# Buffers for turned and flat planes in a hybrid decoder layer: four and three in place of two and four

## The chip, the cores and the metric

The kernel runs on one core of one Trainium2 chip. The metric is device time in microseconds of one execution; lower is better. Before the change the median of three runs is 2429.04 us (2428.55 to 2429.09).

## What is computed

One decoder layer over 256 tokens of width 2048, all in float32: a SwiGLU, two token mixers in parallel (retention and sliding-window attention), a second SwiGLU, and a final RMS norm. A conditioning vector `c` gives nine rows of shifts, scales and gates by the product with `w_ada`.

```python
def token_mixing(h, w_in, w_ret_branch, w_swa_branch, w_out, sinks):
    rq, rk, rv, rg, sq, sk, sv, gl_ret, gl_swa = jnp.split(h @ w_in, IN_SPLITS, axis=-1)
    ...
    ro = retention_chunkwise(rq, rk, rv)
    ro = ro * lax.rsqrt(jnp.mean(ro * ro, axis=-1, keepdims=True) + NORM_EPS)
    ro = (jax.nn.silu(rg.astype(jnp.float32)) * ro.reshape(b, s, RET_V_W)).astype(h.dtype)
    y_ret = ro @ w_ret_branch
    so = swa_with_sinks(...)
    y_swa = so @ w_swa_branch
    merged = jax.nn.sigmoid(gl_ret) * y_ret + jax.nn.sigmoid(gl_swa) * y_swa
    return merged @ w_out

def reference(x, c, w_ada, ...):
    c_act = jax.nn.silu(c)
    for l in range(DEPTH):
        mod = (c_act @ w_ada[l] + b_ada[l]).reshape(b, N_MOD, D_MODEL)
        h = modulate(rms_norm(x, norm_ffn1[l]), mod[:, 0], mod[:, 1])
        x = x + 0.5 * mod[:, 2][:, None, :] * swiglu(h, w_ffn1_gu[l], w_ffn1_down[l])
        h = modulate(rms_norm(x, norm_mix[l]), mod[:, 3], mod[:, 4])
        x = x + mod[:, 5][:, None, :] * token_mixing(h, ...)
        h = modulate(rms_norm(x, norm_ffn2[l]), mod[:, 6], mod[:, 7])
        x = x + 0.5 * mod[:, 8][:, None, :] * swiglu(h, w_ffn2_gu[l], w_ffn2_down[l])
    return rms_norm(x, norm_final)
```

## The kernel before

**Products.** Every float32 factor is split into a high part (`wh` of a weight, `hh` or `a` of an activation) and the rest (`wl`, `hl` or `a`), and each product is made of three: high by high, rest by high, high by rest (L342, L343, L344). Weights come as tiles `raw` of 128 x 4 x 512 (1 MB, L327, four buffers). Each is split in two pieces of 128 x 1024: ACT casts the high part (L350), DVE subtracts it from the raw tile for the low part (L352), into three buffers each. A piece feeds 12 matmuls: two rows of weights, two halves of the tokens, three products. A chunk of 512 output columns of a 2048-deep product takes 96 matmuls. The branch products take their activations from a slot and split them in pairs as they go: ACT casts (L385), DVE subtracts (L386), into the pool `asp` with two buffers.

**Turning.** Results with tokens on partitions have to be turned before the next product. Most are turned by DMA, in halves of 16 bits. `turn_by_dma` has three steps: `apart` copies the low and the high 16-bit words of a 128 x 512 tile into two flat planes on ACT (L452, pool `flat`); `turn` has SP issue a transpose for each plane (L458, pool `back`); `together` weaves the two turned planes back into the 32-bit destination on ACT (L466). The steps are spread over the weight loads that follow: `later` puts the two token halves of a chunk at steps 1 and 2 (`apart`), 6 and 7 (`turn`) and 9 (`together`), one step for each weight tile, and there are four tiles to a chunk, so the transposes of a chunk stand just behind the first `together` of the chunk ahead. `later_by_pairs` does the same for the four merged tiles of the first half of the branches: all four `apart` at once, and then pair by pair.

**Conditioning.** Beside the products DVE multiplies rows of `w_ada` with `silu(c)` and sums them (L206), four passes of 512 columns to a load of 1 MB (L201). In the mixing part these loads share the four `raw` buffers with the weights.

**Order.** SP's instructions stay in the order in which they are written. Those of PE, DVE and ACT are put in order by the framework, which plays the program through a model of the engines, buffers included, while it builds it; on the chip each engine then takes its list strictly in turn. POOL issues a few loads (gates, constants) from a scratch of descriptors in SBUF.

**Stages**, by the trace: the first SwiGLU to about 770 us, the norm and the way into mixing to 880, window queries, retention queries and keys to about 1090, retention values to 1150, gates and the retention gate to 1327, the branch products of the first half to about 1418, gates to 1509, branch products of the second half to 1600, then `w_out`, and the second SwiGLU from about 1720.

## Time and profile before

| what | us |
|---|---|
| median of three runs | 2429.04 |
| the profiled execution | 2432.27 |
| its span in the profile | 2430.5 |
| PE busy | 2379.1 |
| DVE busy | 1702.6 |
| ACT busy | 1284.1 |
| POOL busy | 5.6 |

The profile is of one execution; its span runs from the first to the last instruction. The engines are PE (matmuls), DVE (vector), ACT (scalar), POOL, and SP, which issues the loads; a row names the line of the kernel, the tile written and the tiles read. "SPq" is SP's queue: its waits are times in which it stood at the head of its list. Busy shares are means over the whole span; what a change in one stage is worth is read from that stage.

### The profile page before, as it was taken

Reading aid. Unit: us, or ns where it says so; the run is one execution under the profiler, and the core shown is the slowest. Engines: PE = TensorE matmul, PEld = TensorE weight load, DVE = VectorE, ACT = ScalarE, POOL = GpSimd, SP = SyncE. Lnnn points to the kernel's source line nnn. Section 1 sums busy time; section 2 is a strip of 40 time slices with the busy share of each in tenths; the row PEclk is TensorE's granted clock in tenths of the full one; section 3 lists DMA queues with packets and bytes.
Section 4 is the critical chain, followed back from the end, with each engine's and each line's share of the span. In section 5 each row is a group of like instructions: output and inputs, shape, how many; then the busy total and the mean of one; then the engine's idle time right before and its main releaser. Section 6 shows DMA issues by size and latency. Waiting matters only on the chain.

```text
span 2430.5 us, 28957 instructions
## 1 busy us (share of the span) xinstructions
PE 2379.1 (98%) x10686; PEld 1938.2 (80%) x10686; DVE 1702.6 (70%) x2741; ACT 1284.1 (53%) x1778; POOL 5.6 (0%) x14
## 2 busy tenths in 40 slices
PE   6999999999999999999999999999999999999998
PEld 4778888888787787778888788887788888888886
DVE  6998787778877668886666676767655555545656
ACT  5544545454545456665555554446555445454544
POOL 0000000000000000000000000000000000000000
PEclk9999999999999999999999999999999999999999
DMA  9988689998875677675677878755687777765563
GB/s 339 338 328 286 217 310 319 363 320 303 304 267 191 242 245 240 210 259 206 241 246 238 278 236 302 277 190 191 214 246 241 242 248 244 256 226 191 185 200 121
DMA packets 305008, 613.76 MB, mean 253 GB/s; under 512 B 70561, under 2 KB 70945, under 8 KB 286049
## 3 DMA queue, kind: packets, MB, share of 16 engines
q1 hardware_dynamic: 303362, 605.25, 73.3%
q0 software_dynamic: 928, 5.61, 0.6%
q8 instruction: 84, 1.38, 0.2%
q10 hardware_dynamic: 576, 1.05, 0.1%
q14 instruction: 58, 0.48, 0.1%
HBM read 595.06 MB, written 2.12 MB: 246 GB/s over the span
## 4 chain that ended last, share of the span: by engine, by line
PE 88%; DVE 4%; ACT 1%; issue 1%; DMA 1%; DVEq 0%; ACTq 0%
PE pa L344 28%; PE pa L343 28%; PE pa L342 28%; DVE wl L352 1%; PE ps L436 1%; ACT wh L350 1%; DMA raw<-in_w_ada_dram 1%; DVE slot L206 1%; DVE t L553 0%; PE pd L960 0%; PE pd L956 0%; DVE slot L874 0%; DVE raw L206 0%; PE ps L1029 0%; ACT hh L562 0%
## 5 line engine op out<-in xcount | busy, mean ns | idle before, releaser
L352 DVE TENSOR_TENSOR wl<-raw,wh 128x1024 fp32r<-128x1024 f32 (+1 forms) x828 | 994.0, 1207 | 584.2 <-ACT wh L350 578.8
L350 ACT CAST wh<-raw 128x1024 fp32r<-128x1024 f32 (+1 forms) x828 | 859.1, 1041 | 976.6 <-PE pa L343 936.1
L342 PE MATMUL pa<-wh,hh 128*128 128x512 f32 x2224 | 870.5, 393 | 3.6 <-ACT wh L350 3.1
L343 PE MATMUL pa<-wh,hl 128*128 128x512 f32 x2224 | 868.6, 391 | 2.4 <-DVE hl L527 1.9
L344 PE MATMUL pa<-wl,hh 128*128 128x512 f32 x2224 | 796.4, 392 | 4.0 <-DVE wl L352 3.7
L344 PEld LDWEIGHTS pa<-wl,hh 128*128 128x128 f32 x2224 | 415.5, 188 | 98.6 <-DVE wl L352 10.6
L342 PEld LDWEIGHTS pa<-wh,hh 128*128 128x128 f32 x2224 | 417.9, 188 | 93.5 <-ACT wh L350 5.0
L343 PEld LDWEIGHTS pa<-wh,hl 128*128 128x128 f32 x2224 | 418.2, 188 | 91.4 <-DVE hl L527 2.6
L343 PE MATMUL pa<-wh,a 128*128 128x512 f32 x992 | 385.3, 390 | 3.5 <-DVE a L386 3.5
L342 PE MATMUL pa<-wh,a 128*128 128x512 f32 x992 | 368.2, 391 | 3.1 <-DVE t L570 1.2
L344 PE MATMUL pa<-wl,a 128*128 128x512 f32 x992 | 367.7, 391 | 0.7 <-DVE wl L352 0.6
L342 PEld LDWEIGHTS pa<-wh,a 128*128 128x128 f32 x992 | 186.5, 188 | 44.0 <-DVE t L570 1.9
L343 PEld LDWEIGHTS pa<-wh,a 128*128 128x128 f32 x992 | 186.9, 188 | 42.9 <-DVE a L386 4.4
L344 PEld LDWEIGHTS pa<-wl,a 128*128 128x128 f32 x992 | 186.5, 188 | 41.0 <-DVE wl L352 2.5
L206 DVE CUSTOM_DVE_ANT_0 slot<-slot,cact 128x512 f32<-128x512 f32 (+1 forms) x252 | 192.8, 813 | 15.4 <-DMA slot<-in_w_ada_dram 15.1
L206 DVE CUSTOM_DVE_ANT_0 raw<-raw,cact 128x512 f32<-128x512 f32 (+1 forms) x260 | 167.1, 695 | 42.6 <-DMA raw<-in_w_ada_dram 30.9
L386 DVE TENSOR_TENSOR a<-slot,a 128x512 fp32r<-128x512 f32 x124 | 84.8, 685 | 14.0 <-ACT a L385 14.0
L385 ACT CAST a<-slot 128x512 fp32r<-128x512 f32 x124 | 76.4, 618 | 14.8 <-PE pa L344 14.7
L466 ACT COPY slot<-back 128x512 uint16<-128x512 uint16 x112 | 74.8, 766 | 0.0
L452 ACT COPY flat<-t 128x512 uint16<-128x512 uint16 x104 | 59.1, 618 | 7.9 <-DVE t L1088 6.3
L206 DVE DVE_READ_ACCUMULATOR2_ANT sums<- 128x1 f32 x512 | 41.9, 82 | 0.0
L486 ACT ACTIVATE pd<-x_sb 128x512 f32<-128x512 f32 x32 | 19.0, 593 | 35.8 <-DVE x_sb L571 32.2
(167 smaller groups left out, 986.6 us busy)
## 6 DMA issues: line engine op xcount, KB each, us to landing
raw<-in_w_ffn_gu_dram SPq DMA_DIRECT2D x152, 1024.0 KB, 5.3
raw<-in_w_in_dram SPq DMA_DIRECT2D x104, 1024.0 KB, 5.6
raw<-in_w_ffn_down_dram SPq DMA_DIRECT2D x88, 1024.0 KB, 5.2
slot<-in_w_ada_dram SPq DMA_DIRECT2D x76, 1024.0 KB, 7.5
raw<-in_w_ada_dram SPq DMA_DIRECT2D x64, 1024.0 KB, 5.9
raw<-in_w_ffn_gu_dram SPq DMA_DIRECT2D x24, 768.0 KB, 6.4
raw<-in_w_swa_branch_dram SPq DMA_DIRECT2D x16, 1024.0 KB, 6.0
raw<-in_w_ret_branch_dram SPq DMA_DIRECT2D x16, 1024.0 KB, 5.2
```

Source lines behind the costliest of these rows:

```text
L206: nc.vector.tensor_tensor_reduce(out=w[:, at], in0=w[:, at], in1=cact[:, at], scale=1.0, scalar=0.0, op0=ALU.mult, op1=ALU.add, accum_out= ...
L342: nc.tensor.matmul(ps, ah[:, j, ts], wh[:, j, :], start=first, stop=False)
L343: nc.tensor.matmul(ps, al[:, j, ts], wh[:, j, :], start=False, stop=False)
L344: nc.tensor.matmul(ps, ah[:, j, ts], wl[:, j, :], start=False, stop=last)
L350: cast.append(nc.scalar.copy(hi, src).ins)
L352: nc.vector.tensor_sub(lo, src, hi.bitcast(F32))
L385: nc.scalar.copy(hi, v)
L386: nc.vector.tensor_sub(lo, v, hi.bitcast(F32))
L436: nc.tensor.transpose(ps[:, j * P : (j + 1) * P], src_of(j), ident)
L452: nc.scalar.copy(planes[:, i, :], words(src)[:, :, i])
L466: nc.scalar.copy(into[:, :, :, i], held["turned"][:, i])
L486: nc.scalar.activation(side_bank(), src, AF.Square, accum_out=dest)
```

## The change

Pool `flat` has three buffers in place of four and pool `back` four in place of two. `turn_by_dma` takes a pool and a tag for its flat planes, which are now a float32 tile of 128 x 512 seen as two planes of 16 bits; the four merged tiles take theirs from the pool of 512-column tiles (`tmp`, tag `t512`, five buffers). The scratch for POOL's descriptors is 2048 in place of 4096 bytes. A flat and a `back` buffer are 2 KB a partition each.

```diff
-    flat = ctx.enter_context(tc.tile_pool(name="flat", bufs=4))
-    back = ctx.enter_context(tc.tile_pool(name="back", bufs=2))
+    flat = ctx.enter_context(tc.tile_pool(name="flat", bufs=3))
+    back = ctx.enter_context(tc.tile_pool(name="back", bufs=4))
...
-    def turn_by_dma(dest, src):
+    def turn_by_dma(dest, src, pool=flat, tag="flat"):
...
         def apart():
-            planes = flat.tile([P, 2, CH], U16, tag="flat", name=nm("flat"))
+            planes = pool.tile([P, CH], F32, tag=tag, name=nm("flat"))
+            planes = planes.bitcast(U16).rearrange("p (i n) -> p i n", i=2)
             with tc.issue_after(cast[-1]):
...
                 if p == 0:
-                    work.append(turn_by_dma(dest, m))
+                    work.append(turn_by_dma(dest, m, tmp, "t512"))
                     continue
...
-    nc = _bacc.Bacc("TRN2", target_bir_lowering=False, num_devices=1, dynamic_dma_scratch_size=4096)
+    nc = _bacc.Bacc("TRN2", target_bir_lowering=False, num_devices=1, dynamic_dma_scratch_size=2048)
```

The number of instructions of each kind and the order on SP and POOL stay as they are; lines below L450 are one further on. What moves is what SP's transposes wait for, and the order on PE, DVE and ACT from the window queries on.

SP where the sliding-window branch begins, before, with the semaphores that each row waits for (DMAHW: the landing of an earlier DMA; DVE, Activation: those engines' progress; `back_10687` and `back_10736` are the turned planes of the third chunk of the retention gate):

```order
L327 DMA raw_10651<-in_w_swa_branch_dram 128x4x512 [waits DMAHW6_49,DMAHW0_49,DVE_49]
L458 DMA_TRANSPOSE back_10687<-flat_10468 128x4x128 [waits DMAHW7_49,Activation_49]
L458 DMA_TRANSPOSE back_10687<-flat_10468 128x4x128
L327 DMA raw_10699<-in_w_swa_branch_dram 128x4x512 [waits DMAHW4_49,DMAHW1_49,DVE_49]
L201 DMA raw_10733<-in_w_ada_dram 128x2048 [waits DMAHW3_49,DMAHW2_49,DVE_49]
L458 DMA_TRANSPOSE back_10736<-flat_10512 128x4x128 [waits Activation_49]
```

The same rows of the change:

```order
L327 DMA raw_10651<-in_w_swa_branch_dram 128x4x512 [waits DMAHW6_49,DMAHW4_49,DVE_49]
L459 DMA_TRANSPOSE back_10687<-flat_10468 128x4x128 [waits DMAHW7_49]
L459 DMA_TRANSPOSE back_10687<-flat_10468 128x4x128 [waits DMAHW0_49]
L327 DMA raw_10699<-in_w_swa_branch_dram 128x4x512 [waits DMAHW1_49,DVE_49]
L201 DMA raw_10733<-in_w_ada_dram 128x2048 [waits DMAHW3_49,DMAHW2_49,DVE_49]
```

The transposes stand where they stood and no longer wait for ACT.

DVE at the same place, before; `raw_10733` is the conditioning load of SP's rows, `t_10591` and `t_10594` are the last chunk of the retention gate:

```order
L1167 TENSOR_TENSOR t_10591<-t_10591,slot_8209 128x512
L352 TENSOR_TENSOR wl_10654<-raw_10651,wh_10653 128x1024
L1167 TENSOR_TENSOR t_10594<-t_10594,slot_8209 128x512
L352 TENSOR_TENSOR wl_10671<-raw_10651,wh_10670 128x1024
L352 TENSOR_TENSOR wl_10702<-raw_10699,wh_10701 128x1024
L206 ISA raw_10733,sums_10800<-raw_10733,cact 128x512
L206 ISA sums_10800 128x1
L352 TENSOR_TENSOR wl_10718<-raw_10699,wh_10717 128x1024
```

The other three passes and then the two activation pairs (L386) follow. Now, from the last pass on:

```order
L206 ISA raw_10733,sums_10800<-raw_10733,cact 128x512
L206 ISA sums_10800 128x1
L1168 TENSOR_TENSOR t_10591<-t_10591,slot_8209 128x512
L352 TENSOR_TENSOR wl_10654<-raw_10651,wh_10653 128x1024
L1168 TENSOR_TENSOR t_10594<-t_10594,slot_8209 128x512
L352 TENSOR_TENSOR wl_10671<-raw_10651,wh_10670 128x1024
L352 TENSOR_TENSOR wl_10702<-raw_10699,wh_10701 128x1024
L352 TENSOR_TENSOR wl_10718<-raw_10699,wh_10717 128x1024
L386 TENSOR_TENSOR a_10693<-slot_6392,a_10693 128x512
```

All four passes are ahead of the gate's last chunk, two weight pieces behind the piece that frees their `raw` buffer (`wl_10573`) where they were five behind it, and the activation pairs have no pass between them and the weights.

DVE in the retention queries, before, just ahead of a conditioning block:

```order
L352 TENSOR_TENSOR wl_7479<-raw_7459,wh_7478 128x1024
L1082 TENSOR_TENSOR t_7380<-pa_7111,small_c 128x4x64 x2
L977 TENSOR_TENSOR mx_7439<-mx_7439,sink_b 128x4
L1087 TENSOR_TENSOR t_7379<-t_7379,t_7380 128x4x64
L1088 TENSOR_TENSOR t_7379<-t_7379,t_7380 128x4x64
L981 TENSOR_SCALAR ng_7443<-mx_7439 128x4
L206 ISA raw_7555,sums_6278<-raw_7555,cact 128x512
```

And now, from the piece that frees the block's buffer on:

```order
L352 TENSOR_TENSOR wl_7334<-raw_7314,wh_7333 128x1024
L984 TENSOR_TENSOR se_7300<-ng_7298,sink_b 128x4
L999 TENSOR_TENSOR sm_7303<-sm_7303,se_7300 128x4
L1000 RECIPROCAL sm_7303<-sm_7303 128x4
L1005 TENSOR_SCALAR a_7285<-a_7285,sm_7303 128x128 x2
L1005 TENSOR_SCALAR a_7285<-a_7285,sm_7303 128x256 x2
L352 TENSOR_TENSOR wl_7391<-raw_7388,wh_7390 128x1024
L206 ISA raw_7555,sums_6278<-raw_7555,cact 128x512
```

The block has moved forward by three weight pieces: before, four pieces and some two dozen small rows stood between `wl_7334` and it, now one piece and five rows.

## The prediction

> **What bounds the kernel now.** I read the busy shares of the page first, then PE by windows, then the timelines of the one stretch that stands out.

> ```profile
> PE 2379.1 (98%) x10686; PEld 1938.2 (80%) x10686; DVE 1702.6 (70%) x2741; ACT 1284.1 (53%) x1778; POOL 5.6 (0%) x14
> ```

> TensorE is busy 98% of the span, so the end moves only where PE stands still or runs slowly. Matmuls overlap in the records, so the number of them in a window says more than busy time. The first rows are consecutive windows, the last one their sum up to 1480 (columns: window, length and PE busy time with instructions, granted clock, DMA share, GB/s).

> ```profile
> 1320.00:1336.00 16.00, 16.00 (x72) 1.00 0.65 217
> 1336.00:1362.00 26.00, 20.96 (x78) 0.87 0.70 232
> 1362.00:1456.00 94.00, 93.56 (x411) 1.00 0.80 270
> 1456.00:1480.00 24.00, 23.75 (x104) 1.00 0.82 291
> 1480.00:1600.00 120.00, 119.83 (x530) 1.00 0.77 270
> 1320.00:1480.00 160.00, 154.27 (x660) 0.98 0.77 262
> ```

> From 1480 to 1600 a 128x512 matmul starts every 120/530 = 0.2264 us. At that pace the 660 of 1320 to 1480 need 149.4 us and took 160: 10.6 us are lost there. The 78 of 1336 to 1362 need 17.7 of 26: **8.3 us** are lost in this place alone, the start of the first sliding-window branch product.

> ```profile
> 1338.78 0.73 PE L342 MATMUL pa<-wh,a 128*128 128x512 f32 x2
> 1343.00 0.79 PE L343 MATMUL pa<-wh,a 128*128 128x512 f32 x1 [3.48 <-DVE a L386]
> 1343.59 0.63 PE L344 MATMUL pa<-wl,a 128*128 128x512 f32 x1
> ...
> 1348.28 0.44 PE L343 MATMUL pa<-wh,a 128*128 128x512 f32 x1
> ```

> PE stands from about 1339 to 1343 for `a`, the low part of an activation pair, and after that its starts are 0.43 us apart until 1348.28: the granted clock of the window falls to 0.87. What was `a` late for? These are DVE and then ACT in the same stretch.

> ```profile
> 1337.30 1.23 DVE L352 TENSOR_TENSOR wl<-raw,wh 128x1024 fp32r<-128x1024 f32 x1 [3.69 <-ACT wh L350]
> 1338.67 0.69 DVE L206 CUSTOM_DVE_ANT_0 raw<-raw,cact 128x512 f32<-128x512 f32 x1
> ...
> 1342.26 1.29 DVE L386 TENSOR_TENSOR a<-slot,a 128x512 fp32r<-128x512 f32 x2
> ```

> ```profile
> 1325.84 2.65 ACT L466 COPY slot<-back 128x512 uint16<-128x512 uint16 x4
> ...
> 1336.21 2.00 ACT L350 CAST wh<-raw 128x1024 fp32r<-128x1024 f32 x2 [2.83 <-DMA raw<-in_w_swa_branch_dram]
> ...
> 1354.26 2.03 ACT L466 COPY slot<-back 128x512 uint16<-128x512 uint16 x3
> ```

> DVE idled 3.69 us for a cast, ACT had idled for a weight load, and `a` stands behind both and behind four conditioning passes. The weight load was late in SP's queue:

> ```profile
> 1312.64 4.89 SPq L327 DMA_DIRECT2D raw<-in_w_swa_branch_dram  x2
> 1327.26 3.29 SPq L458 DMA_TRANSPOSE back<-flat  x2
> 1330.66 0.53 SPq L327 DMA_DIRECT2D raw<-in_w_swa_branch_dram  x1
> 1331.29 0.44 SPq L201 DMA_DIRECT2D raw<-in_w_ada_dram  x1
> ...
> 1342.37 0.34 SPq L201 DMA_DIRECT2D raw<-in_w_ada_dram  x1
> 1355.68 2.50 SPq L458 DMA_TRANSPOSE back<-flat  x2
> ```

> SP issued nothing from 1317.5 to 1327.26, nor from 1342.7 to 1355.68. Both times it ends when ACT has joined the turned planes of the chunk before (L466), which frees a `back` buffer. Over the run SP's own waits are:

> ```profile
> SPq L458 <- ACT slot L466: 103.9, 9, 13.7
> ...
> SPq L458 <- ACT a L385: 14.1, 1, 14.1
> ...
> SPq L458 <- ACT t L1166: 11.4, 1, 11.4
> ```

> The three rows are one wait: a transpose at the head of SP's queue, held for ACT's count, 129.4 us in eleven pieces.

> **The change part by part.** *Four `back` buffers.* A transpose now needs the buffer of two chunks ago, and no transpose waits for ACT (the order's rows show it). At the place above SP goes on at 1317.5, and the weights that it loaded at 1330.66 and 1358.30 follow as their `raw` buffers come free, some 7 us earlier. ACT's idle 2.83 and DVE's 3.69 us end, and with them the 8.3 us of PE, clock included: **-8.3**. The last row of the sum has a second, smaller case, the transposes of the merged planes at 1456.83: 104 matmuls need 23.5 of 24 us, **-0.5**. The rest of the 10.6 is 1.8 us by difference and 0.95 by the 411 of 1362 to 1456 (a matmul on a window's edge is counted twice); no such wait lies there, and I leave it.

> Nothing is saved by the other eight pieces of the wait, which lie before 1320: up to three weight pieces stand ready for PE there, and it was not held.

> *What is late next.* DVE now takes the conditioning block of the same place two weight pieces after the one that frees its buffer, not five. The freeing piece and PE's first matmul of the branch are these:

> ```profile
> 1322.38 1.22 DVE L352 TENSOR_TENSOR wl<-raw,wh 128x1024 fp32r<-128x1024 f32 x1
> 1327.63 0.39 PE L342 MATMUL pa<-wh,a 128*128 128x512 f32 x1
> ```

> ```profile
> raw<-in_w_ada_dram SPq DMA_DIRECT2D x64, 1024.0 KB, 5.9
> ```

> Freed at 1323.6 and landed 5.9 us on, at 1329.5; four passes at 0.62 (1338.67 and its like start 0.61 apart) to 1332.0; then L1167 (0.69) and a piece (1.22) to 1333.9. PE does 12 matmuls a piece, 2.72 us; its third piece starts at 1333.1 and needs the low half 0.45 us on, at 1333.5. So 0.4 us are lost, nothing if the load lands a microsecond sooner, and 1.9 if it takes the 7.4 us that it took at 1331.29 among transposes. I take **+0.7** (0 to 2).

> *The moved conditioning blocks of the query and key chunks.* From 900 to 1100 DVE's order brings each block to one or two weight pieces behind the one that frees its buffer. The same spacing is what 1100 to 1240 has now. First windows, then DVE's waits for these loads in each (us, times, longest):

> ```profile
> 900.00:1100.00 200.00, 200.00 (x1064) 157.10 (x1061) 167.78 (x399) 133.37 (x284) 0.00 (x0) 1.00 0.73 242
> 1100.00:1240.00 140.00, 140.00 (x660) 115.81 (x659) 94.11 (x196) 75.64 (x122) 0.00 (x0) 1.00 0.65 226
> ```

> ```profile
> DVE raw L206 <- DMA raw<-in_w_ada_dram: 7.8, 7, 2.3
> ```

> ```profile
> DVE raw L206 <- DMA raw<-in_w_ada_dram: 8.4, 6, 2.2
> ```

> With the short spacing a block costs DVE 8.4/6 = 1.4 us of standing, and PE lost nothing by it. From 900 to 1100 there are 12 blocks (48 passes by the view of L206), so 12 x 1.4 = 16.8, 9.0 more than the 7.8 now. DVE (third pair of numbers: 167.78 busy) has 32.2 us free there, 24.4 beside these waits. So likeliest nothing reaches PE; but the stage is fuller (84% against 67%), and single blocks will bunch. Bounds: 0, and if each load lands 5.9 us after its release with only 2.9 busy behind it (the shortest I add up in the new order), 12 x 3 = 36, 3.8 over what is free and some 10 with DVE's other waits. I take **+0.5** (0 to 10), near the row of the same spacing.

> *Three flat buffers.* A plane is written into the buffer whose transposes were issued a chunk before.

> ```profile
> L458 SPq DMA_TRANSPOSE back<-flat x112: 1194/1286/3522, 367.1 to 2153.6; - x112
> ...
> DMA to landing us min/median/max: 2.4/5.5/9.6
> ```

> Issued before a chunk's 21.8 us (96 matmuls of 0.2264) are over, they have landed. Cover: that SP is not held. If it is, ACT stands at L452 and PE after it, by up to the 9.6 us of the slowest landing; without ACT's wait in SP's queue I put it at nothing. *Merged planes in the 512-column pool*: four of its five tiles are held from the copies at 1425.5 to SP's transposes some 20 us later, and no other instruction of that stretch takes one: nothing. *Half the scratch of POOL's loads*: the closest user of such a load,

> ```profile
> 1574.41 0.55 POOL L283 DMA_DIRECT2D row<-gate_d  x1 [2.29 <-DMA gate_d<-t]
> ...
> L570 DVE TENSOR_TENSOR t<-pa,row x8: 678/682/692, 1643.4 to 1692.7; 128x512 f32<-128x512 f32 x8
> ```

> comes 69 us later. Even a load of several times the 9.6 us above is hidden: nothing.

> Sum: -8.3 - 0.5 + 0.7 + 0.5 = **-7.6 us**. The profiled execution took 2432.27 us (span 2430.5, 1.8 around it); the median of the runs is 2429.04, 3.2 less. The sum taken from the profiled execution gives 2424.7, and less 3.2 it is **2421.4 us**.

> On the clock: eleven starts at 0.43 in place of 0.23 cost 2.2 of the 8.3 us. [...]

> **The rivals.**
> *All of it comes back.* If the late loads also caused the 1.8 us up to 1456 and no new wait arises, 10.6 go: 2429.04 - 10.6 = 2418.4. For it: those windows follow the stall directly. Against: they are branch products too, and the second branch pair (1480 to 1600) is free of loss only because nothing else is on DVE there.
> *The stall only changes its name.* Activation pairs have two buffers, so `a` cannot be made until PE ends with the pair before; if this and not SP's lateness sets 1338.78, the gap stays near 4 us. For it: PE waits for `a`, not for weights. Against: DVE's idle 3.69 us just before, ended by a cast. It gives back 0 to 3 us; 2427.5.
> *DVE becomes the bound from 900 to 1100.* A block at the head of DVE's queue holds the window softmax behind it, and PE's transposes of it have no buffer ahead. From the point where a block waits about 3 us the free time is used up: +10 there, and if two of the gaps exceed 3.5 us, twice 2.2 for the clock: -7.6 - 0.5 + 14.4 = +6.3, so 2435.3. For it: 84% busy, 20 us more or less of new waiting. Against: at the same spacing 1.4 us a block, and loads that are no longer bunched behind a held SP should land sooner.
> *The change does not do what it says* (transposes wait elsewhere): the order shows no ACT wait on any of them; I give it to the second rival.

> **How the numbers follow.** Forecast 0.60, all back 0.17, renamed stall 0.14, DVE the bound 0.09. What a measurement can tell from no change is 0.2%, 4.9 us: faster is below 2424.2, slower above 2433.9. Of the forecast's 0.60 some 0.03 fall above 2424.2 and of the renamed stall about 0.01 below: faster 0.75. Slower is the larger part of the last rival, 0.07; the same keeps 0.18. The forecast's own range is 2419.4 to 2424.4. The range of 8 in 10 reaches down to the middle of the second case, 2418, and up over most of the renamed stall, 2428; it leaves out DVE as the bound and the extremes.

> **What would show it.** In the changed kernel's SP waits no transpose waits for ACT. SP issues a transpose within 1 us of the loads ahead of it at the start of the branch. PE between 1320 and 1480 holds some 690 matmuls where 660 stood, at a granted clock of 1.00, and no PE wait for `a` is over 1.5 us. From 900 to 1100 DVE's waits for conditioning loads grow from 7.8 to 12 to 20 us, and PE shows no wait for L436 or L352. I am wrong if PE shows gaps of over 1 us before 1300, if the granted clock dips anywhere after the start, or if the wait for `a` stays.

## The result, and the profile after

| kernel | median, us (range, runs) | the kernel before in the same set | ratio, 95% interval |
|---|---|---|---|
| changed | 2424.23 (2422.49 to 2425.89, 10) | 2428.95 | 0.998 (0.9971 to 0.999) |
| changed, again in a later set | 2422.88 (2421.72 to 2424.65, 6) | 2430.13 | 0.997 (0.9958 to 0.9982) |

The change makes the kernel faster by 4.7 us in one set and 7.3 in another, and the two intervals overlap; 7.6 were forecast. The profiled execution of the first set took 2425.12 us (span 2423.3), 7.2 less than that of before. Not all of this is the change. These are windows of PE at the start, of before and then of after (window, length and busy time with instructions, clock, DMA share, GB/s):

```profile
1.00:62.00 61.00, 42.26 (x142) 1.00 0.95 346
62.00:900.00 838.00, 826.73 (x3680) 1.00 0.81 287
900.00:1100.00 200.00, 200.00 (x1064) 1.00 0.73 242
```

```profile
1.00:62.00 61.00, 44.26 (x153) 1.00 0.99 358
62.00:900.00 838.00, 826.85 (x3680) 1.00 0.83 291
900.00:1100.00 200.00, 200.00 (x1057) 1.00 0.71 221
```

In the first 62 us this execution started 11 matmuls more, 2.5 us at 0.2264. No row of the order has moved there: that is how two executions differ. Up to 900 they go alike. From 900 to 1100 seven matmuls **fewer** start: the change loses 1.6 us there. The gain stands where it was forecast, at the branch products (the rows of before are in the prediction):

```profile
1336.00:1362.00 26.00, 24.95 (x110) 1.00 1.04 247
...
1456.00:1480.00 24.00, 23.96 (x106) 1.00 0.78 270
1480.00:1600.00 120.00, 119.84 (x533) 1.00 0.73 253
1320.00:1480.00 160.00, 157.28 (x688) 1.00 0.86 269
```

From 1336 to 1362 there are 110 matmuls where 78 stood, at a granted clock of 1.00 instead of 0.87. Over 1320 to 1480 it is 688 against 660, 28 x 0.2264 = 6.3 us. A second profile of the changed kernel, from the later set, has more in two of these windows:

```profile
1336.00:1362.00 26.00, 26.00 (x116) 1.00 0.84 262
...
1320.00:1480.00 160.00, 159.30 (x700) 1.00 0.82 275
```

That is 40 x 0.2264 = 9.1 us. The table puts stages side by side. It takes the same weight products of PE (third products, L344, counted in order) in each trace; the heads give their times in the trace of before, and each figure is how much longer the stretch took than there, in us:

| kernel | to 62 | 62 to 890 | 890 to 1110 | 1110 to 1300 | 1300 to 1480 | 1480 to 1620 |
|---|---|---|---|---|---|---|
| changed | -2.6 | +0.1 | +1.9 | 0.0 | -6.4 | -0.1 |
| changed, again | -3.1 | -0.2 | +1.9 | +0.4 | -9.1 | -0.5 |

The loss is the same in both executions, the gain is not. From 62 us on the columns come to -4.5 and -7.5, close to the 4.7 and 7.3 of the medians, though each profile is one execution.

The wait that the change was to remove, 129.4 us in eleven pieces, is gone from the list of SP's waits of after. All that its transposes still wait for ACT is this:

```profile
SPq L459 <- ACT wh L350: 1.0, 1, 1.0
SPq L459 <- ACT t L437: 0.9, 1, 0.9
```

**Where the two profiles of one kernel differ by 12 matmuls.** First PE, then DVE, then SP, in the first profile of after:

```profile
1350.45 0.50 PE L343 MATMUL pa<-wh,a 128*128 128x512 f32 x1 [1.05 <-DVE a L386]
...
1366.46 0.73 PE L344 MATMUL pa<-wl,a 128*128 128x512 f32 x2 [1.21 <-DVE wl L352]
```

```profile
1346.11 0.69 DVE L206 CUSTOM_DVE_ANT_0 raw<-raw,cact 128x512 f32<-128x512 f32 x1 [3.21 <-DMA raw<-in_w_ada_dram]
...
1362.73 0.69 DVE L206 CUSTOM_DVE_ANT_0 raw<-raw,cact 128x512 f32<-128x512 f32 x1 [2.15 <-DMA raw<-in_w_ada_dram]
```

```profile
1337.49 0.34 SPq L201 DMA_DIRECT2D raw<-in_w_ada_dram  x1
1337.88 3.34 SPq L459 DMA_TRANSPOSE back<-flat  x2
```

And in the second profile, SP and DVE at the same place:

```profile
1337.14 0.34 SPq L201 DMA_DIRECT2D raw<-in_w_ada_dram  x1
1337.54 2.56 SPq L459 DMA_TRANSPOSE back<-flat  x2
```

```profile
1342.65 0.69 DVE L206 CUSTOM_DVE_ANT_0 raw<-raw,cact 128x512 f32<-128x512 f32 x1
```

A conditioning load with two transposes right behind it came to DVE 8.6 us after its issue in the one execution (1337.49 to 1346.11, DVE standing 3.21 us), and at most 5.5 in the other (1337.14 to 1342.65, DVE not waiting). The load and the transposes behind it are the same in both, so the transposes do not explain the difference. DMA as a whole was slower in the first: from 1332 to 1346 its engines were busier by the profile's count (1.06 against 0.86) and moved less (224 GB/s against 263). First the first profile, then the second:

```profile
1332.00:1346.00 14.00, 14.00 (x63) 1.00 1.06 224
```

```profile
1332.00:1346.00 14.00, 14.00 (x63) 1.00 0.86 263
```

The two weight loads of that stretch, on either side of the conditioning load, took 7.6 and 8.3 us to land in the first and 5.1 and 5.4 in the second. Why DMA was slower in one execution stays open. Behind the blocked pass stand the weight pieces and the activation pair, and PE waits 1.05 and 1.21 us for them. In the second profile neither wait is there. Here are PE's waits from 1320 to 1480 in each (us, times, longest), the first profile first:

```profile
PE pa L344 <- DVE wl L352: 1.6, 2, 1.2
PE pa L343 <- DVE a L386: 1.0, 1, 1.0
```

```profile
PE pa L344 <- DVE wl L352: 0.4, 1, 0.4
PE pa L342 <- DVE slot L1184: 0.3, 1, 0.3
```

**Where 1.9 us are lost.** PE shows no wait from 900 to 1100. What changed is the list of PE itself. The logits of a window are four matmuls: two halves of 64 rows each (`pd`, two banks), a 128-column (L956) and a 256-column product (L960). One window in the order of before:

```order
L956 MATMUL pd_8112<-slot_6209,slot_6392 128x128
L956 MATMUL pd_8113<-slot_6209,slot_6392 128x128
L960 MATMUL pd_8112<-slot_6209,slot_6392 128x256
L960 MATMUL pd_8113<-slot_6209,slot_6392 128x256
```

and after, where the lines are one further on:

```order
L957 MATMUL pd_8112<-slot_6209,slot_6392 128x128
L961 MATMUL pd_8112<-slot_6209,slot_6392 128x256
L342 MATMUL pa_7934<-wh_8011,hh_4136 128x512
L343 MATMUL pa_7934<-wh_8011,hl_4137 128x512
L436 MATMUL ps_8051<-small_c,a_7835 128x128
L957 MATMUL pd_8113<-slot_6209,slot_6392 128x128
L961 MATMUL pd_8113<-slot_6209,slot_6392 128x256
```

In five of the 16 windows other matmuls stand between whole halves now, in three before. PE's timeline for a window with its halves together (before), and for one half by itself (after); each of these products leaves two records (128 of `pd` for the 64 products of 16 windows):

```profile
994.54 0.50 PE L956 MATMUL pd<-slot,slot 64*128 64x128 f32 x4
994.86 0.61 PE L960 MATMUL pd<-slot,slot 64*128 64x256 f32 x4
995.40 0.33 PE L1024 MATMUL ps<-t,slot 128*64 128x128 f32 x2
```

```profile
951.31 0.49 PE L957 MATMUL pd<-slot,slot 64*128 64x128 f32 x2
951.64 0.59 PE L961 MATMUL pd<-slot,slot 64*128 64x256 f32 x2
952.16 0.44 PE L1025 MATMUL ps<-t,slot 128*64 128x128 f32 x4
```

Both halves together hold PE for 0.86 us (994.54 to 995.40), one half alone for 0.85 (951.31 to 952.16). A parted window costs 0.84 us more, and two more of them 1.7. The busy time of PE in the logits alone (its windows with tile `pd` as filter; the first pair is PE) says the same, 1.82 us, of before and then after:

```profile
880.00:1110.00 230.00, 19.06 (x128) 10.66 (x128) 16.51 (x32) 0.00 (x0) 1.00 0.71 235
```

```profile
880.00:1110.00 230.00, 20.88 (x128) 11.67 (x128) 16.64 (x32) 0.00 (x0) 1.00 0.75 231
```

Counted from each start to the next over the whole stretch from 890 to 1110, the logits hold PE 1.7 us longer than before, the weight products next to small products 0.3 longer, and all else 0.1 less. That is the whole 1.9.

### The profile page after: what moved, and what is told of

Same layout as the page of the kernel before. It is cut to its first block, busy times and chain, and to the rows that moved or that the text cites. A ratio compares the mean times of both kernels' runs of the same rounds, so it can differ in the third digit from the quotient of the medians.

```text
span 2423.3 us, 28965 instructions
## 1 busy us (share of the span) xinstructions
PE 2377.0 (98%) x10686; PEld 1937.4 (80%) x10686; DVE 1700.6 (70%) x2736; ACT 1286.6 (53%) x1783; POOL 5.7 (0%) x14
## 3 DMA queue, kind: packets, MB, share of 16 engines
q10 hardware_dynamic: 576, 1.05, 0.1%
## 5 line engine op out<-in xcount | busy, mean ns | idle before, releaser
L352 DVE TENSOR_TENSOR wl<-raw,wh 128x1024 fp32r<-128x1024 f32 (+1 forms) x828 | 994.9, 1208 | 573.7 <-ACT wh L350 569.1
L350 ACT CAST wh<-raw 128x1024 fp32r<-128x1024 f32 (+1 forms) x828 | 859.8, 1041 | 964.4 <-PE pa L343 950.7
L342 PE MATMUL pa<-wh,hh 128*128 128x512 f32 x2224 | 870.0, 392 | 3.4 <-ACT wh L350 2.9
L343 PE MATMUL pa<-wh,hl 128*128 128x512 f32 x2224 | 868.9, 391 | 2.4 <-DVE hl L528 1.9
L344 PE MATMUL pa<-wl,hh 128*128 128x512 f32 x2224 | 796.5, 392 | 4.1 <-DVE wl L352 3.9
L342 PEld LDWEIGHTS pa<-wh,hh 128*128 128x128 f32 x2224 | 417.9, 188 | 93.7 <-ACT wh L350 4.2
L344 PEld LDWEIGHTS pa<-wl,hh 128*128 128x128 f32 x2224 | 415.1, 188 | 97.2 <-DVE wl L352 10.2
L343 PEld LDWEIGHTS pa<-wh,hl 128*128 128x128 f32 x2224 | 418.2, 188 | 91.7 <-issue 3.0
L343 PE MATMUL pa<-wh,a 128*128 128x512 f32 x992 | 384.1, 389 | 1.0 <-DVE a L386 1.0
L344 PE MATMUL pa<-wl,a 128*128 128x512 f32 x992 | 366.9, 390 | 2.2 <-DVE wl L352 2.2
L342 PE MATMUL pa<-wh,a 128*128 128x512 f32 x992 | 367.2, 390 | 1.2 <-DVE t L571 1.2
L344 PEld LDWEIGHTS pa<-wl,a 128*128 128x128 f32 x992 | 185.9, 188 | 42.4 <-DVE wl L352 4.4
L342 PEld LDWEIGHTS pa<-wh,a 128*128 128x128 f32 x992 | 186.1, 188 | 41.2 <-DVE t L571 1.9
L343 PEld LDWEIGHTS pa<-wh,a 128*128 128x128 f32 x992 | 186.3, 188 | 40.1 <-DVE a L386 1.7
L206 DVE CUSTOM_DVE_ANT_0 slot<-slot,cact 128x512 f32<-128x512 f32 (+1 forms) x252 | 192.9, 814 | 13.9 <-DMA slot<-in_w_ada_dram 13.8
L206 DVE CUSTOM_DVE_ANT_0 raw<-raw,cact 128x512 f32<-128x512 f32 (+1 forms) x260 | 167.3, 695 | 48.4 <-DMA raw<-in_w_ada_dram 38.0
L386 DVE TENSOR_TENSOR a<-slot,a 128x512 fp32r<-128x512 f32 x124 | 84.9, 685 | 13.6 <-ACT a L385 13.6
L385 ACT CAST a<-slot 128x512 fp32r<-128x512 f32 x124 | 76.4, 618 | 14.8 <-PE pa L344 14.7
L206 DVE DVE_READ_ACCUMULATOR2_ANT sums<- 128x1 f32 x512 | 42.2, 82 | 0.0
L487 ACT ACTIVATE pd<-x_sb 128x512 f32<-128x512 f32 x32 | 19.0, 593 | 34.7 <-DVE x_sb L572 32.2
## 6 DMA issues: line engine op xcount, KB each, us to landing
raw<-in_w_ffn_gu_dram SPq DMA_DIRECT2D x152, 1024.0 KB, 5.3
raw<-in_w_in_dram SPq DMA_DIRECT2D x104, 1024.0 KB, 5.3
raw<-in_w_ffn_down_dram SPq DMA_DIRECT2D x88, 1024.0 KB, 5.2
slot<-in_w_ada_dram SPq DMA_DIRECT2D x76, 1024.0 KB, 7.6
raw<-in_w_ada_dram SPq DMA_DIRECT2D x64, 1024.0 KB, 5.1
raw<-in_w_swa_branch_dram SPq DMA_DIRECT2D x16, 1024.0 KB, 5.4
raw<-in_w_ret_branch_dram SPq DMA_DIRECT2D x16, 1024.0 KB, 5.1
```

The source lines that it names most:

```text
L206: nc.vector.tensor_tensor_reduce(out=w[:, at], in0=w[:, at], in1=cact[:, at], scale=1.0, scalar=0.0, op0=ALU.mult, op1=ALU.add, accum_out= ...
L342: nc.tensor.matmul(ps, ah[:, j, ts], wh[:, j, :], start=first, stop=False)
L343: nc.tensor.matmul(ps, al[:, j, ts], wh[:, j, :], start=False, stop=False)
L344: nc.tensor.matmul(ps, ah[:, j, ts], wl[:, j, :], start=False, stop=last)
L350: cast.append(nc.scalar.copy(hi, src).ins)
L352: nc.vector.tensor_sub(lo, src, hi.bitcast(F32))
```

## The experiments

The same table for the experiments, by their number in the text (one profiled execution each; the first column, where each was 2.1 to 3.5 us ahead of before, is left out):

| experiment | 62 to 890 | 890 to 1110 | 1300 to 1480 | 1480 to 1620 |
|---|---|---|---|---|
| 1, two `back` buffers again | +0.7 | +0.1 | -1.4 | 0.0 |
| 2, other buffers in one part | +0.5 | -0.2 | -9.2 | -0.2 |
| 3, logits as written | -0.2 | +2.2 | -6.9 | +4.1 |
| 4, one half after the other | +1.2 | +3.1 | -9.3 | -0.4 |
| 5, halves parted | +2.3 | +5.8 | -9.3 | -0.2 |
| 6, changed, passes later | +0.1 | +1.9 | -8.1 | +1.5 |
| 7, before, passes later | +1.7 | +0.4 | -4.8 | +2.3 |
| 8, as 2, passes later | 0.0 | -0.2 | -8.4 | +1.3 |
| 9, changed, halves beside | -0.3 | +0.7 | -9.3 | -0.5 |
| 10, as 2, halves beside | -0.2 | -0.4 | -9.2 | +0.1 |

Experiments 1 and 7 have the order of before from 62 to 890 and are 0.7 and 1.7 us over it there: so far do two executions of the same work differ. Most of experiment 7's 1.7, and of experiment 5's 2.3, is a stretch at half clock near 654 us (shown below, at the clock). At the start the trace of before is the odd one, since experiment 1 with the same order is 2.5 us ahead of it too.

**1. The two buffers back.** The changed kernel with

```diff
-    back = ctx.enter_context(tc.tile_pool(name="back", bufs=4))
+    back = ctx.enter_context(tc.tile_pool(name="back", bufs=2))
```

> The changed kernel with pool back at two buffers again; three flat buffers, merged planes in the 512-column pool and the halved scratch stay. Order on every engine is then that of the kernel before. Theory (the wait of SP's transposes is the whole change, the other three edits are worth nothing): 2429.0, within 0.5 of the kernel before; PE again stands some 3.5 us for `a` at the start of the first sliding-window branch product and holds some 78 matmuls in those 26 us; the 16 window logits of four matmuls cost 17.45 us of PE as before. Rival (the flat and merged planes carry a part of the gain): 2424 to 2427.

Measured 2429.10 us, the kernel before 2430.07, ratio 0.9999 (0.999 to 1.0007). The order of every engine is that of before again, and so is the stall:

```profile
1340.76 0.50 PE L343 MATMUL pa<-wh,a 128*128 128x512 f32 x1 [3.38 <-DVE a L386]
1341.10 0.40 PE L344 MATMUL pa<-wl,a 128*128 128x512 f32 x1
1341.33 0.39 PE L343 MATMUL pa<-wh,a 128*128 128x512 f32 x1
...
1342.41 0.63 PE L344 MATMUL pa<-wl,a 128*128 128x512 f32 x1
1342.84 0.63 PE L342 MATMUL pa<-wh,a 128*128 128x512 f32 x1
...
1345.40 0.43 PE L344 MATMUL pa<-wl,a 128*128 128x512 f32 x1
```

The whole gain hangs on `back`; with two of its buffers the three other edits change nothing. The half clock shows here too (starts 0.43 apart from 1342.41 on, a granted clock of 0.93 from 1336 to 1362 against 0.87 before), but the first matmuls behind the gap still run at full pace, and it ends at 1345.40. In this execution the stretch lost 1.4 us less than in the profile of before; the stall's own size varies.

**2. Other buffers for the turned planes of one part alone.** The kernel before, with these lines; the retention gate and the merged tiles pass `True`:

```diff
-            turned = back.tile([P, 2, KB, P], U16, tag="back", name=nm("back"))
+            if into_tmp:
+                turned = tmp.tile([P, CH], F32, tag="t512", name=nm("back"))
+                turned = turned.bitcast(U16).rearrange("p (i k n) -> p i k n", i=2, k=KB)
+            else:
+                turned = back.tile([P, 2, KB, P], U16, tag="back", name=nm("back"))
```

> The kernel before (two back buffers, four flat, full scratch), but the turned planes of the retention gate and of the merged tiles lie in the pool of 512-column tiles, so that SP's transposes do not wait for ACT in that part alone. PE's order up to the branch products is that of the kernel before, window logits included. Theory: the stall of 7.3 and the 0.65 of the merged planes go, and the 1.9 us lost from 985 to 1088 do not come: 2421.5 (2420.5 to 2423). Rival (four back buffers all along the mixing part are needed, since the nine other waits of SP count too): 2424 or more.

2421.37 us against 2430.07, ratio 0.9966 (0.9954 to 0.9978). Of SP's eleven waits the seven before 1070 stay, 82 us, and two shorter ones come at the retention gate (SPq L462 for L470: 91.4 us in all nine). They cost nothing: from 890 to 1110 this kernel takes as long as before (-0.2). PE's list from 900 to 1100 is that of before, its logits are busy 19.06 us again, and the loss there does not come. The window of its branch products holds 701 matmuls, 41 more than before:

```profile
1320.00:1480.00 160.00, 159.40 (x701) 1.00 0.83 275
```

**3 and 4. The logits' order forced.** The changed kernel with PE's order held as written around the four matmuls, once as they stand, once with the two of one half ahead of the two of the other:

```diff
-        with tc.high_priority(offset=300):
+        with tc.manual_schedule(engines={mybir.EngineType.PE}):
```

> The changed kernel with the four matmuls of a window's logits kept in written order on PE, the two 64-row halves side by side, for all 16 windows (side by side in the changed kernel for all but five or so). Theory (the 1.9 us from 985 to 1088 are the logits' order: 0.856 us for a window whose halves stand side by side, 1.70 for one whose halves run one after the other, five of these in the changed kernel and three before): logits fall from 19.1 us of PE to 14 to 16, and the kernel from 2424.2 to 2420.5 (2419 to 2421.5). Rival (DVE's conditioning blocks make the 1.9): no change, 2424.2.

> The changed kernel with the suspected cost raised: one half's two matmuls, then the other half's two, for all 16 windows. Theory: 16 windows of 1.70 us are 27.2 us of PE against 19.1 now, so 2432.3 (2431 to 2433.5). Rival (DVE's conditioning blocks make the 1.9): 2424.2, since PE would have the same number of the same matmuls.

Both missed. The first took 2423.01 us (ratio 0.9976), the second 2423.97 (0.9977): neither can be told from the changed kernel. (The profiled execution of the first took 2428.37 us, the longest of its eleven, with 4.1 us lost from 1480 to 1620 that its median doesn't show: a wait of 2.77 us at 1544 and 3.4 us at half clock behind it.) In the second the halves were written one after the other with nothing between, and PE still ran them beside each other: 19.11 us busy in `pd`, against 20.88 for the changed kernel. So the rival was not confirmed; the experiment had not raised the cost that it meant to raise. It is other work between the halves that parts them, not their order. In the first the logits fell further, to 18.17 us. Yet from 890 to 1110 both kernels took longer than the changed one, by 0.3 and 1.2 us. Without the raised priority the scheduler put single weight products between logits and other small products. PE's timeline in the first:

```profile
1021.08 0.39 PE L343 MATMUL pa<-wh,hl 128*128 128x512 f32 x1
1021.31 0.40 PE L344 MATMUL pa<-wl,hh 128*128 128x512 f32 x1
1021.64 0.37 PE L957 MATMUL pd<-slot,slot 64*128 64x128 f32 x1
...
1022.49 0.50 PE L342 MATMUL pa<-wh,hh 128*128 128x512 f32 x1
1022.82 0.39 PE L343 MATMUL pa<-wh,hl 128*128 128x512 f32 x1
1023.05 0.40 PE L344 MATMUL pa<-wl,hh 128*128 128x512 f32 x1
```

Weight products start 0.23 us apart; the last one ahead of a logit holds PE for 0.33, and so does the first one behind. That is 0.1 us at each side of a change. From 850 to 1115 us PE goes from weight products to small products and back 52 times in each of these kernels, and 43 times in the changed one. Counted from start to start over the stretch of 890 to 1110, the same 778 weight products hold PE 2.5 and 2.4 us longer than there, against the 2.6 and 1.6 us that the logits gave back.

The two sides are not alike for every small product. That of L436, 128 x 128 in the trace, has the 0.1 us on one side alone: in the changed kernel a weight product ahead of it holds PE for 0.23 us, as if nothing changed, but one behind it for 0.32 (medians of 21). What makes the 0.1 us on either side was not tested.

**5. The halves parted by other work.** The changed kernel, the second half at the common priority:

```diff
-        with tc.high_priority(offset=300):
-            for ps, hs in zip(both, halves):
+        for i, (ps, hs) in enumerate(zip(both, halves)):
+            with tc.high_priority(offset=300 * (1 - i)):
```

> The changed kernel with the second half of every window's logits left at the common priority, so that other matmuls stand between the two halves on PE in all 16 windows (6 in the changed kernel, 4 before). Theory (a half that runs without its partner beside it costs PE 0.85 us, which is what both cost side by side): ten more windows of 0.84 are 8.4 us, 2432.6 (2430 to 2434). Rival (DVE's conditioning blocks make the 1.9 us from 985 to 1088): 2424.2.

2427.03 us, ratio 0.9987 (0.9978 to 0.9995): 2.8 over the changed kernel's first median, which is of another set, and a third of what was expected. From 890 to 1110 PE took 3.9 us more than in the changed kernel (+5.8 for +1.9), not the rival's nothing. That it is less than half of 8.4 the order explains: the late half of one window often stands right beside the early half of the next, and those run together (four records of L960 in 0.60 us at 915.18, where the two of one half take 0.59 at 995.53). The logits' busy time rose by 2.5 us, and most of the rest is weight products next to small products, 1.4 us:

```profile
880.00:1110.00 230.00, 23.38 (x128) 12.97 (x128) 17.60 (x32) 0.00 (x0) 1.00 0.75 226
```

**6, 7 and 8. No conditioning passes at the start of the branches.** In the changed kernel, in the kernel before, and in that of experiment 2, the passes pause for 16 half tiles and then come at 1.25 times the pace:

```diff
     def tick():
+        if pace["skip"]:
+            pace["skip"] -= 1
+            if pace["skip"] == 0:
+                pace["rate"] *= 1.25
+            return
...
+    pace["skip"] = 16
     for p in range(2):
```

> The changed kernel without conditioning passes for 16 half weight tiles from the first sliding-window branch on, made up behind by a pace of 1.25. Theory (the waits that took the stall's place, 1.2 us at 1350 and 1.9 at 1366 to 1379, come from conditioning blocks whose loads land late at the head of DVE's list): both go, 2421.5 (2420.5 to 2423). Rival (the two buffers of activation pairs set those waits): they stay, 2424.2; or the passes made up later cost as much, 2424.

> The kernel before with the same passes left until later; SP's transposes wait for ACT as before. Theory (the gap of 3.5 us before `a` is late weights by SP's wait plus four conditioning passes, 2.5 us, ahead of `a`): about 1 us of gap is left and no half clock, some 5 to 6.5 of the 8.3 us go, 2423.3 (2422 to 2425). Rival (the passes ahead of `a` alone make the stall): all goes, 2421. Rival (SP's wait alone makes it): the gap stays near 3.5 us and the clock dips, 2428 to 2429.

> The kernel before with the turned planes of the retention gate and the merged tiles in the pool of 512-column tiles (2421.4 alone) and the passes left until later. Theory: of the 1.2 us that PE still loses at the second product the most goes: 2420.5 (2419.5 to 2421.5). Rival: the passes made up later hold PE in the second half of the branches: 2422 or more.

They took 2426.97 (0.9987), 2426.96 (0.9986) and 2423.15 us (0.9971), with 2430.45 for the kernel before. All three missed the forecast time, and the profiles give one reason for it. At the start of the branches the passes' absence did what it should: 116 matmuls from 1336 to 1362 in the first of them, none of the waits at 1350 and 1366. But the passes made up later hold PE in the second half of the branches. Two rows of that kernel's windows:

```profile
1336.00:1362.00 26.00, 26.00 (x116) 1.00 0.89 222
...
1480.00:1600.00 120.00, 119.07 (x527) 1.00 0.74 255
```

Six fewer than the changed kernel's 533 there; the table has +1.5 for -0.1. Its profiled execution (2424.63) was also among the quicker of its runs, so its profile does not account for all of its median. The kernel before with the pause is the one that tells something on the stall. Its rows of PE and DVE, and SP's waits:

```profile
1338.71 0.50 PE L348 MATMUL pa<-wh,a 128*128 128x512 f32 x1 [0.80 <-DVE a L391]
```

```profile
1335.69 2.36 DVE L357 TENSOR_TENSOR wl<-raw,wh 128x1024 fp32r<-128x1024 f32 x2 [3.45 <-ACT wh L355]
```

```profile
SPq L463 <- ACT slot L471: 119.8, 10, 15.0
```

SP still waits for ACT, DVE still stands 3.45 us for the cast (3.69 before), and PE's gap is 0.80 us instead of 3.48, with no half clock behind it (granted clock 1.00): 111 matmuls from 1336 to 1362 in place of 78, 7.5 us. Late weights alone do not make the stall; late weights **and** four passes between them and `a` do. Either one taken away brings most of it back. What the passes then cost later leaves 4.8 us of it by 1480 and 2.5 by 1620.

**9, 10 and 11. Halves kept beside each other at their priority.** The changed kernel, and the kernel of experiment 2 (there with an offset of 1000), and the changed kernel again beside them:

```diff
-        with tc.high_priority(offset=300):
+        with tc.manual_schedule(engines={mybir.EngineType.PE}), tc.high_priority(offset=300):
```

> The changed kernel with the four matmuls of a window's logits kept in written order on PE and at their raised priority: no window has its halves wholly apart (five in the changed kernel), eight have the first half's small product by itself, and PE changes from weight products to logits or back some three times more, where keeping the order without the priority had changed 13 times more. Theory (the 1.9 us from 985 to 1088 are windows whose halves run apart): logits cost 17.4 us of PE as before the change, against 19.1, less 0.2 for the changes: 1.5 us under the changed kernel of the same call. Rival (DVE's conditioning blocks make the 1.9): no difference from it.

> The kernel before with the turned planes of the retention gate and of the merged tiles in the pool of 512-column tiles, and a window's four logit matmuls in written order at a priority of 1000: 11 windows side by side, none wholly apart. Theory: logits fall from 17.45 to 15.5 us of PE, less 0.3 for three more changes between kinds of matmul: 1.6 under the 2421.4 of the same kernel without it, 2419.8 (2419 to 2421), some 4 under the changed kernel of the same call. Rival (the changes between kinds take it all back, as they did when the order was kept without the priority): 2421.4.

> The changed kernel once more, for a comparison on the same chip: 0.998 of the kernel before, 4.5 us under it.

2421.44 us (ratio 0.9962), 2420.28 (0.9958) and 2422.88 (0.997), with 2430.13 for the kernel before. The logits of the first are busy 19.20 us, 1.7 less than in the changed kernel, and it is 1.44 us faster in the same set, where 1.5 was forecast. Its range (2420.09 to 2422.73) overlaps that of the changed kernel (from 2421.72), so the medians alone would not settle it; the stretch from 890 to 1110, +0.7 for +1.9 twice, and the logits' row do:

```profile
880.00:1110.00 230.00, 19.20 (x128) 10.86 (x128) 16.63 (x32) 0.00 (x0) 1.00 0.74 231
```

The second is the fastest of all, 2.6 us under the changed kernel with no run in common (2419.89 to 2421.08). Its logits fell to 17.01 us. Whether that adds anything to experiment 2 stays open: the medians are 1.1 us apart, in different sets, and the stretch of the logits is 0.2 us shorter where 1.6 was forecast. From start to start the logits do hold PE 1.9 us less there than in experiment 2, but the weight products hold it 0.5 longer and the products with the values (`ps<-t,slot`) 1.1 longer. In three windows the logits, at their higher priority, now stand in the middle of those products, which then hold PE for 1.16 us instead of 0.81. So most of the gain is taken back, as the rival said, and two thirds of that by parted value products.

## Why the prediction was right or wrong

**The stall, -8.3: right.** 78 matmuls became 110 and 116 in the two profiles, 7.2 and 8.6 us, the clock stayed at 1.00, and with two buffers the stall is back. The working named late weights, the cast and four passes in DVE's list; experiment 7 shows that the passes were as necessary as SP's wait. The claim that eight of the eleven pieces of the wait cost nothing is borne out for seven of them by experiment 2, which leaves them in and is as fast at the branches as any (-9.2); around the eighth, at 1295, PE of before shows no wait.

**The clock.** In the trace of before the granted clock is 0.50 from 1342 to 1348, at the end of the 3.48 us gap and in the stretch of half pace behind it. The prediction counts half pace for gaps over 3.5 us with DVE as the bound; no run shows that bound. A gap of 3.38 us was followed by half pace as well, and gaps of 1.21, 1.05 and 0.80 at the branches were not. But in experiment 3 a gap of 2.77 us was, and in experiments 5 and 7 one of only 1.21 us, with a second of 0.40 behind it, near 652 us. The other traces have these two gaps as well (the first up to 1.79 us) and keep the full clock there. These are the 12 us around them, in experiment 7 and then in the kernel before:

```profile
650.00:662.00 12.00, 10.39 (x38) 0.86 0.91 346
```

```profile
650.00:662.00 12.00, 10.39 (x44) 1.00 0.73 255
```

So the clock fell near these two gaps in two executions and not in the others. At which gaps it falls was not tested, and the 2.2 us that the prediction gave to the clock are those of one execution: in experiment 1 the seven starts at 0.43 us cost 1.4.

**The merged planes, -0.5: right**, 106 and 108 matmuls for 104, 0.5 to 0.9 us; experiment 1, with two `back` buffers, has 104 again.

**The new wait, +0.7 (0 to 2): right mechanism, wrong place and too small a bound.** At 1327 to 1334, where it was worked out, PE starts 33 matmuls before and after. The blocks at 1346 and 1362 did it, 2.6 us of PE's waits in one execution and 0.7 in another. The step that failed is "landed 5.9 us on", one landing time for every block and every execution. It held for the load of the place that was worked out (issued at 1321, 5.8 us in both), and the next load took at most 5.5 us in the second execution. In the first, where DMA as a whole was slower, it took 8.6. The text had 7.4 us for its upper end, at that one place only. Of the eight traces with the long wait at the branches gone and the passes in their place, six come to -9.1 to -9.3 there and two (the first of the changed kernel, and experiment 3) to -6.4 and -6.9.

**The conditioning blocks of 900 to 1100, +0.5 (0 to 10): the size within the bounds, the mechanism wrong.** DVE's waits for these loads went from 7.8 to 8.6 us in the first profile and 10.8 in the second, not to 12 to 20, and PE waited for nothing. The 1.9 us, the same in both executions, came from a list that the prediction had not costed: PE's own. The step that failed is taking the order's moves on PE at no price. The instructions are the same in number, but a half without its partner takes as long as both (0.85 us and 0.86).

**Three flat buffers, merged planes, half the scratch, 0: right** by experiment 1. (A chunk of 96 matmuls at 0.2264 us takes 21.7 us, not 21.8, which changes nothing.)

**The sum.** -8.3, -0.5, +0.7, +0.5 make -7.6. At the branches that is -8.1, the new wait in it. The second trace has -9.1 there and +1.9 at the logits: the gain was forecast 1 us too small and the loss ahead of it 1.4 too small, so that the 7.3 us of that set come so near to the forecast in part by luck. The first trace has -6.4 and +1.9: there the gain was forecast 1.7 us too large as well, and 4.7 us came where 7.6 were forecast. Of the 2.7 us between the two at the branches, 1.9 are PE's new waits themselves. The renamed stall and DVE as the bound did not come. "All of it comes back" came near at the branches, 9.1 to 9.3 of the 10.6 in most traces; the loss at the logits kept it from the total. One sign of being wrong, a gap of PE of over 1 us before 1300, could not serve as one: four such gaps stand in the trace of before (at 119, 655, 782 and 801 us, 1.07 to 1.51), and the same four in that of after.

## What to carry to other kernels

A wait is worth what it holds at its last place: here most of eleven pieces were free and one cost some 8 us, because it met four passes in the next engine's list. When a change of buffers lets a scheduler lay out the lists anew, compare the list of the bound engine too, pair by pair, and not only those of the engines around it. And a term that rests on one landing time needs a second execution before its size means much.
